# Five stages of a float32 decoder layer with other operand orders on TensorE

## The chip, the cores and the metric

The kernel runs on one core of one Trainium2 chip. A core has TensorE (PE, with its weight loads shown apart as PEld), VectorE (DVE), ScalarE (ACT), GpSimd (POOL) and SyncE (SP), which here issues the DMAs. The metric is device time in microseconds of one execution. The comparison that counts is the changed kernel against the kernel before, on the same chip.

## The reference

One layer of a hybrid decoder, float32, 256 tokens behind 16 learned meta tokens (272 columns in all), width 2048. What matters for this change is the chain of weight products:

```python
proj = xn @ w_in                      # q, k, v, gates of both branches
o_fox = forgetting_attention(...)     # 8 heads of 128
o_gla = gated_linear_attention(...)   # 4 heads, value width 512
y = sigmoid(gate_fox) * (o_fox @ w_o_fox) + sigmoid(gate_gla) * (o_gla @ w_o_gla)
h = h + y @ w_out
h = h + square(relu(xn2 @ w1)) @ w2   # w1: 2048 x 8192, w2: 8192 x 2048
out = rmsnorm(h)[16:]
```

All weights are used once, by 256 or 272 token columns, and come from HBM as float32.

## The kernel before

Everything is kept transposed: channels on the 128 partitions, tokens along the free dimension. A float32 value is split in two float32r parts, an upper part (hi) and the remainder (lo), and a product is hi·hi + hi·lo + lo·hi. The activations of a block of 128 channels lie as two runs in SBUF, hi tokens and lo tokens, with a gap that each operand sets for itself (AT_OG, AT_Y, AT_X2, AT_A); `x[k]` is a view of 128 x 2 x 256.

The weights come as blocks of 128 output channels by 2048 input channels (`stream()` lists them in order of use). `next_weights` loads one block in two halves of 8 input blocks: SP issues the DMA into `raw`, ScalarE casts it to `whi` (L120), VectorE subtracts to get `wlo` (L121). `raw`, `whi` and `wlo` have 5 buffers each, so up to two and a half blocks are prepared ahead of TensorE.

One output block of 128 channels is one `gemm2`: 16 input blocks, and for each one `mac2` (L135 to L137), which is two matmuls into one PSUM bank of 512 float32 columns. The first has `whi` as weights and streams both runs of the activations, 512 columns (hi·hi into columns 0 to 255, hi·lo into 256 to 511). The second has `wlo` as weights, streams the 256 hi columns and adds to columns 0 to 255. Each matmul has a weight load of its own. Here such two matmuls are called a pair. `total` or `add_residual` then adds the two halves of the bank with ScalarE and VectorE while TensorE is at the next block.

The stages that the change touches, in order of time:

- `gate()` is a `gemm2` over `xt` (the normalised input), with a sigmoid behind it. Four gates are made ahead, while the last steps of the attention heads (`later`, run by `issued()` after each product) are still open; the other 28 come in the loop over `j0`.
- In that loop each output block has one `gemm2` over `og` (the linear attention's output): 16 in all.
- The output projection: 16 `gemm2` over `y`.
- The MLP in four groups `g`: 16 `gemm2` over `x2` (first matrix; `relu2` squares the result and splits it into `a`), then 16 over `a` (second matrix). In group 3 the last NL = 4 output blocks of the second matrix are computed by code of their own, first all `wlo` products (L845), then the `whi` products for one half of the tokens after the other (L854: 2 x 128 columns).

The scheduler keeps each engine's instructions in the order of its own simulation of the program; the PE order is that of the code but for the `later` steps.

Of the kernel before, what the change touches and what calls it, by code (L numbers as in the profile page):

```python
# [16 lines left out]
P = 128  # L17
# [48 lines left out]
def trunk(ctx: ExitStack, tc: tile.TileContext, hT, w_small, w_all, consts, w_alpha2, out):  # L66
# [3 lines left out]
    def nm(s):  # L70
        serial[0] += 1
        return f"{s}_{serial[0]}"
# [35 lines left out]
    def weight_half(c, i, hi=None):  # L108
# [14 lines left out]
        return hi, lo, step  # L123

    def next_weights(keep_hi=None):
        c = chunk[0]
        chunk[0] += 1
        parts = []
        for i in range(2):
            hi, lo, step = weight_half(c, i, None if keep_hi is None else keep_hi[:, HK * i : HK * (i + 1), :])  # L130
            step(0, HK)
            parts.append((hi, lo))
        return lambda k: (parts[k // HK][0][:, k % HK, :], parts[k // HK][1][:, k % HK, :])
# [4 lines left out]

    def gemm2(w, x, k0=0, nk=KT):

        ps = bank(pg, "ps")
        for k in range(nk):
            hi, lo = w(k0 + k)
            mac2(ps, hi, lo, x[k], k == 0, k == nk - 1)
        issued()
        return ps
# [580 lines left out]

    def gate():
        t = total(gemm2(next_weights(), xt))
        nc.gpsimd.tensor_tensor(t, t, rbt, op=ALU.mult)  # L730
        s = late.tile([P, NT], F32, tag="gate", name=nm("gate"), bufs=6)
        nc.scalar.activation(s, t, AF.Sigmoid)
        return s

    ahead = [gate() for _ in range(4)]
    flush()
# [3 lines left out]
    for j0 in range(0, KT, 2):  # L740
# [5 lines left out]
        for j in range(2):  # L746
            t = total(gemm2(next_weights(), og))
            nc.vector.tensor_tensor(t, gates[2 * j + 1], t, op=ALU.mult)
            nc.vector.tensor_tensor(yf[:, j0 + j, :], gates[2 * j], t, op=ALU.add)
# [38 lines left out]
    for j in range(KT):  # L788
        add_residual(j, gemm2(next_weights(), y))
        nc.scalar.activation(x2[j][:, 0, :], ht[:, j, :], AF.Identity, scale=gain(1, j))  # L790
# [167 lines left out]
```

## Time and profile before

| what | value |
|---|---|
| median of the two runs shown | 1636.05 us (1634.11 to 1637.98) |
| span of the profiled execution | 1632.3 us, 3.75 us below that median |
| pairs in `mac2` | 3424 (1952 over x and x2, 960 over a, 256 over og, 256 over y, 128 of the attention's output), in a total of 9996 PE records |
| busy VectorE, ScalarE | 1033.6 us (63%), 788.5 us (48%) |
| HBM read | 289.19 MB, 178 GB/s over the span |

A row of the timeline gives start, length, engine, line, operation, output and inputs, their shapes, and how many instructions are merged. The length of a matmul in a row goes from its start to the modelled end, and matmuls overlap in the array; what one of them costs in a stream is the distance from its start to the start of the next. A row of the stages gives the length of the stage and each engine's busy time in it with the number of instructions. A row of the groups gives the total busy time, the mean in nanoseconds of one, and the idle time ahead of them with what ended it.

### The profile page before, as it was taken

What the parts mean: (1) busy time and instruction counts of PE and PEld (TensorE: products, weight loads), DVE (VectorE), ACT (ScalarE), POOL (GpSimd) and SP (SyncE); (2) the same over time, 40 slices, a digit from 0 to 9 for tenths busy, and PEclk for the clock granted to TensorE, in tenths of its full rate; (3) what the DMA queues carried; (4) which work ended last, traced back from release to release, by engine and by line L of the source; (5) the groups of instructions that cost most, each with busy time, mean ns of one, the idle gap of its engine ahead of it and who ended that gap; (6) DMA issues with size and microseconds to landing.
All of it is one profiled execution on the core that took longest, in us unless ns stands there. A gap on an engine that the chain in (4) does not pass through costs nothing.

```text
span 1632.3 us, 25617 instructions
## 1 busy us (share of the span) xinstructions
PE 1614.8 (99%) x9996; PEld 1448.8 (89%) x9996; DVE 1033.6 (63%) x1591; ACT 788.5 (48%) x1217; POOL 93.4 (6%) x146
## 2 busy tenths in 40 slices
PE   9999999999999999999999999999999999999997
PEld 7999999999998888888888888888888888888886
DVE  6767657476655555555677766566655776567655
ACT  6555444454445444444555444444444444444563
POOL 1000000010000000000011000000000000000022
PEclk9999999999999999999999999999999999999998
DMA  9444455455455565655555555655566656565662
GB/s 290 143 151 157 159 167 163 160 189 160 157 161 169 187 190 187 188 188 189 188 187 189 185 186 188 188 188 188 181 196 186 191 184 191 187 190 185 188 196 66
DMA packets 90266, 292.97 MB, mean 179 GB/s; under 512 B 9096, under 2 KB 21648, under 8 KB 89888
## 3 DMA queue, kind: packets, MB, share of 16 engines
q1 hardware_dynamic: 87552, 288.88, 55.8%
q8 instruction: 78, 1.28, 0.3%
q10 hardware_dynamic: 2416, 1.33, 0.3%
q0 software_dynamic: 176, 1.12, 0.2%
q14 instruction: 44, 0.36, 0.1%
HBM read 289.19 MB, written 2.11 MB: 178 GB/s over the span
## 4 chain that ended last, share of the span: by engine, by line
PE 97%; DVE 1%; DMA 1%; ACT 0%; issue 0%; SPq 0%; DVEq 0%; ACTq 0%
PE ps L136 50%; PE ps L137 26%; PE psa L155 5%; PE psa L154 5%; PE psa L153 5%; PE ps L854 1%; PE ps L339 1%; DMA h<-hT_dram 1%; PE pa L501 1%; PE ps L845 0%; PE ps L346 0%; PE po L565 0%; DMA raw<-w_all_dram 0%; PE pz L399 0%; PE po L566 0%; PE pq L663 0%
## 5 line engine op out<-in xcount | busy, mean ns | idle before, releaser
L121 DVE TENSOR_TENSOR wlo<-raw,whi 128x1024 fp32r<-128x1024 f32 x522 | 639.9, 1226 | 502.9 <-ACT whi L120 501.3
L120 ACT CAST whi<-raw 128x1024 fp32r<-128x1024 f32 x522 | 547.6, 1049 | 750.9 <-PE ps L136 507.0
L136 PE MATMUL ps<-x,whi 128*128 128x512 f32 x1952 | 688.2, 396 | 0.0
L137 PE MATMUL ps<-x,wlo 128*128 128x256 f32 x1952 | 549.5, 282 | 0.0
L136 PEld LDWEIGHTS ps<-x,whi 128*128 128x128 f32 x1952 | 367.0, 188 | 84.1
L137 PEld LDWEIGHTS ps<-x,wlo 128*128 128x128 f32 x1952 | 368.8, 189 | 0.0
L136 PE MATMUL ps<-a,whi 128*128 128x512 f32 x960 | 336.3, 395 | 0.0
L137 PE MATMUL ps<-a,wlo 128*128 128x256 f32 x960 | 268.5, 280 | 0.0
L136 PEld LDWEIGHTS ps<-a,whi 128*128 128x128 f32 x960 | 180.0, 188 | 42.2
L153 PE MATMUL psa<-x,whi 128*128 128x272 f32 x640 | 187.1, 292 | 2.1 <-DVE ri L196 2.1
L154 PE MATMUL psa<-x,wlo 128*128 128x272 f32 x640 | 184.9, 289 | 0.0
L155 PE MATMUL psa<-x,whi 128*128 128x272 f32 x640 | 184.8, 289 | 0.0
L137 PEld LDWEIGHTS ps<-a,wlo 128*128 128x128 f32 x960 | 181.2, 189 | 0.4
L153 PEld LDWEIGHTS psa<-x,whi 128*128 128x128 f32 x640 | 120.4, 188 | 2.8 <-issue 2.1
L154 PEld LDWEIGHTS psa<-x,wlo 128*128 128x128 f32 x640 | 120.5, 188 | 0.2
L155 PEld LDWEIGHTS psa<-x,whi 128*128 128x128 f32 x640 | 120.6, 188 | 0.1
L136 PE MATMUL ps<-og,whi 128*128 128x512 f32 x256 | 90.3, 395 | 0.0
L136 PE MATMUL ps<-y,whi 128*128 128x512 f32 x256 | 89.8, 395 | 0.0
L766 POOL TENSOR_TENSOR acc<-acc,hsq 128x256 f32<-128x256 f32 x26 | 29.5, 1134 | 775.6 <-ACT hsq L765 775.6
L137 PE MATMUL ps<-og,wlo 128*128 128x256 f32 x256 | 71.8, 281 | 0.0
L137 PE MATMUL ps<-y,wlo 128*128 128x256 f32 x256 | 71.7, 281 | 0.0
L165 DVE TENSOR_TENSOR evt<-ps,evb 128x256 f32<-128x256 f32 x158 | 66.1, 418 | 0.0
(262 smaller groups left out, 1387.0 us busy)
## 6 DMA issues: line engine op xcount, KB each, us to landing
raw<-w_all_dram SPq DMA_DIRECT2D x537, 512.0 KB, 4.3
raw<-w_all_dram SPq DMA_DIRECT2D x7, 384.0 KB, 6.3
h<-hT_dram SPq DMA_DIRECT2D x1, 1100.0 KB, 10.0
negc<-fdram POOLq DMA_DIRECT2D x1, 1088.0 KB, 6.0
out_dram<-h SPq DMA_DIRECT2D x3, 256.0 KB, 2.6
out_dram<-h ACTq DMA_DIRECT2D x3, 256.0 KB, 3.1
h<-hT_dram SPq DMA_DIRECT2D x1, 550.0 KB, 7.3
raw<-w_all_dram SPq DMA_DIRECT2D x2, 256.0 KB, 4.4
```

What stands on the lines that cost most here:

```text
L120: nc.scalar.copy(hi[:, k, :], r)
L121: nc.vector.tensor_tensor(lo[:, k, :], r, hi[:, k, :].bitcast(F32), op=ALU.subtract)
L136: nc.tensor.matmul(ps, hi, x, start=first, stop=False)
L137: nc.tensor.matmul(ps[:, 0:NT], lo, x[:, 0, :], start=False, stop=last)
L153: nc.tensor.matmul(ps[:, 0:n], hi, x[:, k, 0, :], start=(k == 0), stop=False)
L154: nc.tensor.matmul(ps[:, 0:n], lo, x[:, k, 0, :], start=False, stop=False)
L155: nc.tensor.matmul(ps[:, 0:n], hi, x[:, k, 1, :], start=False, stop=(k == KT - 1))
L165: nc.vector.tensor_tensor(t, ps[:, 0:NT], b, op=ALU.add)
L339: nc.tensor.matmul(ps, hi, x[:, k, :, NM:NA], start=st, stop=False)
L501: nc.tensor.matmul(dst, k[:, a, :], q[:, a, :], start=(a == 0), stop=(a == 1))
L766: nc.gpsimd.tensor_tensor(acc, acc, sq, op=ALU.add)
L854: nc.tensor.matmul(ps[:, NT:], w(k)[0], a[k][:, :, tok], start=(k == 0), stop=(k == KT - 1))
```

## The change

Products, inputs and outputs stay the same; each of five stages forms them in another order.

- The four gates made ahead use `mac2_halves`: per input block four matmuls, for each half of the tokens one of 2 x 128 columns with `whi` and one of 128 columns with `wlo`. The weights are loaded in the order hi, lo, hi, lo.
- The products over `og` use `gemm2_runs`: for each half of the weights, first the eight matmuls of 512 columns with `whi`, then the eight of 256 with `wlo`.
- The output projection uses `mac2_thirds`: three matmuls of 256 columns (hi·hi, hi·lo, lo·hi), with `whi` loaded twice.
- MLP group 1 uses `mac2_back`: both matmuls stream their columns from the last to the first, and write the PSUM columns from the last to the first.
- MLP group 2 uses `mac2_lo_back`: only the `wlo` matmul goes backwards.
- MLP group 3 (but for the last four output blocks) uses `paired_weights`: the hi and lo weights of an input block lie in one tile, alternating element by element, so that ScalarE and VectorE write, and the weight loads read, every second element. The tiles are cut so that each of the two tags holds four input blocks with both parts, and a half is made by two casts and two subtractions of 512 elements in place of one each of 1024. The DMAs are the same.

```diff
+    def paired_weights():
+        c = chunk[0]
+        chunk[0] += 1
+        parts = []
+        for i in range(2):
+            raw = wp.tile([P, HK * P], F32, tag="raw", name=nm("raw"), bufs=RAW)
+            nc.sync.dma_start(raw, w_all[c][:, i * HK * P : (i + 1) * HK * P])
+            r = raw.rearrange("p (q k m) -> p q k m", q=2, m=P)
+            for q, tag in enumerate(("whi", "wlo")):
+                t = wp.tile([P, HK // 2, P, 2], F32R, tag=tag, name=nm(tag))
+                nc.scalar.copy(t[:, :, :, 0], r[:, q])
+                nc.vector.tensor_tensor(t[:, :, :, 1], r[:, q], t[:, :, :, 0].bitcast(F32), op=ALU.subtract)
+                parts.append(t)
+        return lambda k: tuple(parts[k // 4][:, k % 4, :, o] for o in range(2))
...
+    def mac2_back(ps, hi, lo, x, first, last):
+        nc.tensor.matmul(ps[:, ::-1], hi, x[:, ::-1, ::-1], start=first, stop=False)
+        nc.tensor.matmul(ps[:, NT - 1 :: -1], lo, x[:, 0, ::-1], start=False, stop=last)
+
+    def mac2_lo_back(ps, hi, lo, x, first, last):
+        nc.tensor.matmul(ps, hi, x, start=first, stop=False)
+        nc.tensor.matmul(ps[:, NT - 1 :: -1], lo, x[:, 0, ::-1], start=False, stop=last)
+
+    def mac2_halves(ps, hi, lo, x, first, last):
+        both = ps.rearrange("p (o t) -> p o t", t=NT)
+        for i in range(2):
+            t = slice(P * i, P * (i + 1))
+            nc.tensor.matmul(both[:, :, t], hi, x[:, :, t], start=first and i == 0, stop=False)
+            nc.tensor.matmul(ps[:, t], lo, x[:, 0, t], start=False, stop=last and i == 1)
+
+    def mac2_thirds(ps, hi, lo, x, first, last):
+        nc.tensor.matmul(ps[:, 0:NT], hi, x[:, 0, :], start=first, stop=False)
+        nc.tensor.matmul(ps[:, NT:], hi, x[:, 1, :], start=False, stop=False)
+        nc.tensor.matmul(ps[:, 0:NT], lo, x[:, 0, :], start=False, stop=last)
+
+    def gemm2_runs(w, x):
+        ps = bank(pg, "ps")
+        for k0 in range(0, KT, HK):
+            for k in range(k0, k0 + HK):
+                nc.tensor.matmul(ps, w(k)[0], x[k], start=(k == 0), stop=False)
+            for k in range(k0, k0 + HK):
+                nc.tensor.matmul(ps[:, 0:NT], w(k)[1], x[k][:, 0, :], start=False, stop=(k == KT - 1))
+        issued()
+        return ps
...
-    ahead = [gate() for _ in range(4)]
+    ahead = [gate(mac2_halves) for _ in range(4)]
...
-            t = total(gemm2(next_weights(), og))
+            t = total(gemm2_runs(next_weights(), og))
...
-        add_residual(j, gemm2(next_weights(), y))
+        add_residual(j, gemm2(next_weights(), y, mac=mac2_thirds))
...
+        weights, mac = ((next_weights, mac2), (next_weights, mac2_back), (next_weights, mac2_lo_back), (paired_weights, mac2))[g]
...
-            ps = gemm2(next_weights(), x2)
+            ps = gemm2(weights(), x2, mac=mac)
...
-            add_residual(j, gemm2(next_weights(), a))
+            add_residual(j, gemm2(weights(), a, mac=mac))
```

`gemm2` and `gate` take the form as an argument (`mac`).

Two places show it in the engines' programs. The first is on PE, where the last attention head ends (`pof` is its output, `pq` the scores of the next) and the first gate made ahead begins (`ps`). Before:

```order
L184 MATMUL pof_5514<-pah_5424,val_5365 128x256
L714 MATMUL pof_5514<-pT_5295,vb_5294 128x144
L715 MATMUL pof_5514<-pc_3631,vc_3627 128x16
L663 MATMUL pq_5522<-fk_5297,fq_5298 128x144
L136 MATMUL ps_5551<-x,whi_5540 128x512
L137 MATMUL ps_5551<-x,wlo_5541 128x256
```

And in the changed kernel:

```order
L229 MATMUL pof_5514<-pah_5424,val_5365 128x256
L759 MATMUL pof_5514<-pT_5295,vb_5294 128x144
L760 MATMUL pof_5514<-pc_3631,vc_3627 128x16
L708 MATMUL pq_5522<-fk_5297,fq_5298 128x144
L166 MATMUL ps_5551<-x,whi_5540 128x2x128
L167 MATMUL ps_5551<-x,wlo_5541 128x128
```

What surrounds the gate stays where it was; the pair has become smaller matmuls, which appear twice per input block.

The second place is on ScalarE, where the weights of MLP group 3 begin to be prepared, still during the second matrix of group 2 (`evb` is the copy in `add_residual`). Before:

```order
L770 COPY evb_14227<-ps_14194 128x256
L120 CAST whi_14336<-raw_14335 128x1024
L120 CAST whi_14380<-raw_14379 128x1024
L770 COPY evb_14276<-ps_14243 128x256
L120 CAST whi_14386<-raw_14385 128x1024
L120 CAST whi_14434<-raw_14433 128x1024
```

And in the changed kernel:

```order
L120 CAST whi_14720<-raw_14719 128x1024
L135 CAST whi_14765<-raw_14763 128x512
L815 COPY evb_14660<-ps_14627 128x256
L135 CAST wlo_14768<-raw_14763 128x512
L135 CAST whi_14773<-raw_14771 128x512
L135 CAST wlo_14776<-raw_14771 128x512
```

One cast per half has become two of half the length, the second into a buffer of the tag `wlo`; the copies out of PSUM keep their places among the halves.

More of the change, by code (lines that the diff above doesn't have):

```diff
@@ L137, in mac2, with gemm2 @@
         nc.tensor.matmul(ps[:, 0:NT], lo, x[:, 0, :], start=False, stop=last)
-    def gemm2(w, x, k0=0, nk=KT):
+    def mac2_back(ps, hi, lo, x, first, last):
[23 more added lines that the diff above has]
+        return ps
+    def gemm2(w, x, k0=0, nk=KT, mac=mac2):
         ps = bank(pg, "ps")
@@ L143, in gemm2 @@
             hi, lo = w(k0 + k)
-            mac2(ps, hi, lo, x[k], k == 0, k == nk - 1)
+            mac(ps, hi, lo, x[k], k == 0, k == nk - 1)
         issued()
@@ L725, in trunk, with gate @@
         fox_head(hd)
-    def gate():
-        t = total(gemm2(next_weights(), xt))
+    def gate(mac=mac2):
+        t = total(gemm2(next_weights(), xt, mac=mac))
         nc.gpsimd.tensor_tensor(t, t, rbt, op=ALU.mult)
```

## The prediction

> **What bounds the kernel now.** I read the page first: engine shares, slices, and the chain that ended last.
>
> ```profile
> span 1632.3 us, 25617 instructions
> ...
> PE 1614.8 (99%) x9996; PEld 1448.8 (89%) x9996; DVE 1033.6 (63%) x1591; ACT 788.5 (48%) x1217; POOL 93.4 (6%) x146
> ...
> PEclk9999999999999999999999999999999999999998
> ...
> PE 97%; DVE 1%; DMA 1%; ACT 0%; issue 0%; SPq 0%; DVEq 0%; ACTq 0%
> ```
>
> TensorE is the chain. Its busy share alone would not say so, because matmul ends are modelled; the chain does, with 97% of the span, and the granted clock gives no slack to win back. Then the table of waits, for the two engines that prepare the weights:
>
> ```profile
> ACT whi L120 <- PE ps L136: 507.0, 340, 3.9
> DVE wlo L121 <- ACT whi L120: 501.3, 470, 3.7
> ```
>
> ScalarE waits 507 us in total for TensorE to hand back a weight buffer, and VectorE 501 us for ScalarE. The suppliers are ahead of the consumer, so the change is priced by what it does to the pace of matmuls. The stages that it touches, by the table of busy times by stretch (a gate loop, the products over og, the projection, MLP groups 1 and 2, and the two matrices of group 3):
>
> ```profile
> 573.52:595.92 22.40, 22.40 (x130) 19.64 (x129) 11.99 (x14) 10.42 (x15) 2.21 (x3) 1.00 0.58 187
> 562.27:573.52 11.25, 11.25 (x67) 9.82 (x65) 7.27 (x10) 4.74 (x6) 0.00 (x0) 1.00 0.55 187
> 808.68:898.47 89.79, 89.79 (x515) 78.60 (x514) 64.53 (x82) 49.31 (x80) 13.48 (x14) 1.00 0.59 187
> 1078.92:1258.53 179.61, 179.61 (x1027) 156.84 (x1026) 114.90 (x160) 80.65 (x112) 0.00 (x0) 1.00 0.60 188
> 1258.53:1438.13 179.60, 179.60 (x1026) 156.84 (x1025) 114.91 (x160) 80.66 (x112) 0.00 (x0) 1.00 0.60 188
> 1438.13:1528.02 89.89, 89.89 (x514) 78.50 (x513) 62.82 (x94) 42.47 (x63) 0.00 (x0) 1.00 0.60 187
> 1528.02:1595.31 67.29, 67.29 (x386) 58.77 (x385) 39.20 (x50) 42.31 (x64) 13.44 (x10) 1.00 0.60 189
> ```
>
> PE is busy in every microsecond of them (first two columns equal). Divided by their pairs: 22.40/64 = 0.350 us for the gates, 11.25/32 = 0.352 for og, 89.79/256 = 0.351 for the projection, 179.61/512 = 0.351 in groups 1 and 2, 89.89/256 and 67.29/192 = 0.351 in group 3. Inside a pair, by the timeline of PE (start, length, line, operation):
>
> ```profile
> 1099.96 0.39 PE L136 MATMUL ps<-x,whi 128*128 128x512 f32 x1
> 1100.19 0.28 PE L137 MATMUL ps<-x,wlo 128*128 128x256 f32 x1
> 1100.31 0.39 PE L136 MATMUL ps<-x,whi 128*128 128x512 f32 x1
> ```
>
> From start to start the 512 columns take 0.23 and the 256 columns 0.12 us: time follows the columns, about 0.457 ns each.
>
> Three rows price the smaller matmuls: the end of the kernel, which has long series of 256 columns (L845 one run with wlo, L854 two runs of 128 with whi), and the attention heads, which have the smallest shapes.
>
> ```profile
> 1595.31 5.86 PE L845 MATMUL ps<-a,wlo 128*128 128x256 f32 x48
> 1601.01 1.80 PE L854 MATMUL ps<-a,whi_last 128*128 128x256 f32 x14
> ...
> 1604.78 8.46 PE L854 MATMUL ps<-a,whi_last 128*128 128x256 f32 x70
> 1613.08 0.28 PE L872 MATMUL pn<-ones,acc 128*128 128x1 f32 x2
> ```
>
> 48 in 5.70 us are 0.1188 each, 70 in 8.30 us are 0.1186 each, every one with a weight load of its own.
>
> ```profile
> 365.55 0.27 PE L701 MATMUL pt<-cons,pr 128*128 128x128 f32 x1
> ...
> 365.99 0.27 PE L705 MATMUL pu<-cons,pr 128*16 128x128 f32 x1
> ...
> 372.25 0.27 PE L183 MATMUL pof<-pal,vah 128*128 128x256 f32 x1
> 372.36 0.28 PE L184 MATMUL pof<-pah,val 128*128 128x256 f32 x1
> 372.48 0.41 PE L714 MATMUL pof<-pT,vb 128*128 128x144 f32 x2
> 372.73 0.29 PE L715 MATMUL pof<-pc,vc 128*128 128x16 f32 x2
> ...
> 372.61 0.31 PEld L715 LDWEIGHTS pof<-pc,vc 128*128 128x128 f32 x2
> 372.84 0.30 PEld L663 LDWEIGHTS pq<-fk,fq 128*128 128x128 f32 x2
> ```
>
> Four transposes of 128 columns take 0.44, 0.11 each. A plain float32 product of 144 columns takes 0.25 (two records). Two weight loads of 128 columns take 0.23, although the products beside them have only 16 columns: a weight load cannot be paced faster than about 0.115, and a lo matmul of 0.119 hides the next one with almost nothing to spare.
>
> **The change, part by part.**
>
> *Gates.* 64 pairs of 0.350 become 64 times two hi matmuls of 2 x 128 columns at 0.1186 (the L854 row is this very shape on the reading side) and two lo matmuls of 128 columns. For the latter no row has float32r. Lower end: half of a 256-column one, 0.059, if the weight loads were free; 2 x (0.1186 + 0.059) = 0.355, +0.3 us in all. Upper end: the plain float32 pace, 0.25/144 x 128 = 0.222; 2 x 0.3406 = 0.681, +21.2 us. I take 0.11, the transposes, nearest in columns and near the pace of the weight loads that here come one per matmul: 2 x 0.2286 = 0.457, +0.107 x 64 = +6.8 us. It lies on the path, since nothing on PE waits in this stage; the `later` steps of the last head only get more time.
>
> *Runs.* The same 256 + 256 matmuls. In a run of eight lo matmuls each weight load must hide under one of 256 columns instead of 512; the L845 row is such a run, at 0.1188 against 0.12 in the pair. Price 0, between -0.5 and +0.5 us (0.002 x 256). If the cover failed and a load of 0.115 lay bare once per lo matmul, it would be +29 us, which that row excludes. The wlo half is asked for later and the whi half handed back earlier, both on the safe side.
>
> *Thirds.* 256 pairs of 0.3507 become three matmuls of 0.1188: 0.3564, +0.0057 x 256 = +1.4 us, between 0 (time by columns alone) and +1.6 (0.119 each). The additional weight loads hide as in the L845 row.
>
> *Backwards.* 512 pairs wholly, 512 in the lo matmul only; no instruction more. No row has a descending operand, so the bounds are rows of pace: above, the 128-column transposes, 0.11/128 = 0.859 ns per column; below, the 0.11 us in which L183 streams 256, 0.43 ns. With 0.859 group 1 pays (768 x 0.859 ns - 0.351) x 512 = +158 us and group 2 (0.220 - 0.118) x 512 = +52 us; with 0.43 they gain 0.021 x 512 = 10.7 and 0.008 x 512 = 4.1 us. I take 0: the columns, lines and banks touched are the same ones, only in descending order, and the nearest row is the same pair ascending.
>
> *Interleaved weights.* 448 pairs; more instructions for ScalarE and VectorE, by the groups:
>
> ```profile
> L120 ACT CAST whi<-raw 128x1024 fp32r<-128x1024 f32 x522 | 547.6, 1049 | 750.9 <-PE ps L136 507.0 <-issue 148.3 <-PE psa L155 84.3
> L287 ACT CAST whi<-raw 128x768 fp32r<-128x768 f32 x7 | 5.8, 832 | 3.9 <-PE ps L339 3.0 <-DMA raw<-w_all_dram 0.9
> ...
> L121 DVE TENSOR_TENSOR wlo<-raw,whi 128x1024 fp32r<-128x1024 f32 x522 | 639.9, 1226 | 502.9 <-ACT whi L120 501.3 <-issue 0.4
> L288 DVE TENSOR_TENSOR wlo<-raw,whi 128x768 fp32r<-128x768 f32 x7 | 6.7, 956 | 3.5 <-PE ps L346 3.0 <-ACT whi L287 0.6
> ```
>
> Going on from 1024 and 768 to 512 elements gives 0.615 for a cast and 0.686 for a subtraction: per block 4 x 0.615 = 2.46 us on ScalarE (2.10 before) and 4 x 0.686 = 2.74 on VectorE (2.45). In the first matrix of group 3 VectorE goes from 62.82 to 67.5 us of 89.89, ScalarE from 42.47 to 48.2: still hidden behind PE. Should VectorE handle every second element at half its pace, a subtraction costs 1.226, the stage needs 62.82 + 16 x 2.45 = 102 us of VectorE, and the cover is gone: +12 us there and +1.3 in the second matrix. The weight load now reads every second element. If its pace stays 0.115, nothing; if it doubles to 0.23, the lo matmul no longer covers the next load and each pair grows by 0.23 - 0.12 = 0.11, +49 us. I take 0, since the nearest row, the same load of as many columns, is below the matmul it hides under. The page "SBUF — State Buffer" of the Trainium skill (Specifications) says that a 16-byte line needs at least two accesses for full bandwidth; steps of two float32 just meet that, so by the page the sum would be the same 0. No trace here shows it.
>
> Sum: 6.8 + 0 + 1.4 + 0 + 0 = +8.2 us on a span of 1632.3, so 1640.5; with the 3.75 us between the span and the median of the runs shown, 1644.3. Its own range, with the gates' ends and the bounds of thirds and runs, is 1636 to 1659.
>
> **The rivals.**
>
> *Descending columns cost time (slower).* Place: every matmul of group 1, and the lo one in group 2. Price: up to +158 and +52 us, 1644 + 210 = 1854. It decides from about 0.504 ns per descending column on (0.457 now): 0.047 ns x (768 + 256) x 512 = 24.6 us, which with the 8.2 is 2%. For it speaks that PE has nothing to hide it behind; against it, that the matmul of two runs (L854) pays nothing for its jump, so the order of addresses is not all that sets the pace. The page "PSUM — Partial Sum Buffer" of the Trainium skill (Specifications) says that lines there have 8 bytes and any non-contiguous pattern slows matmuls significantly; if a descending run counts as such, this rival is what it gives. No run so far has such an output.
>
> *Interleaving costs time.* Through VectorE +13.5 us, 1658; through the weight loads +49 us, 1693. For it: loads of 0.115 have only about 4 ns of cover under the lo matmul. Against: the suppliers' large waits, and that the load's pace goes by columns.
>
> *The orders do nothing at all,* the gates included: the 128-column lo matmuls cost half of the 256. Then about 1636. Against it stand the two weight loads in 0.23.
>
> *Faster.* If a changed order let all 2048 pairs stream at 0.43 ns, it would be 2048 x 0.021 = 43 us less, 1644 - 43 = 1601. Only one row has that pace.
>
> **How the numbers follow.** Forecast 0.58, 1644; descending columns at the full price 0.18, 1854; interleaving, or a small part of the descending price, 0.18, from 1658 to 1693, of which 0.12 beyond 2%; nothing at all 0.04, 1636; faster 0.02, 1601. The range 1632 to 1700 takes in the first, third and fourth case, 0.80, its upper end the third case with some of the gates' upper end. By a bound of 2% (33 us, about what a measurement of this kernel can tell from no change): faster 0.02, same 0.58 + 0.06 + 0.04 = 0.68, slower 0.18 + 0.12 = 0.30.
>
> **What would show it.** In the changed trace: the gates' four matmuls in 0.457 us per input block; og and the projection within 2% of 0.351; groups 1 and 2 179.6 us each; group 3 without waits of PE for VectorE, and its pairs at 0.351. A gate step near 0.68 would put the 128-column float32r matmul at the plain float32 pace; a group 1 far above 180 us while group 2 grows by a third as much would be the descending rival; a lo matmul of 0.23 in group 3 alone the weight-load one. The forecast is wrong if any of the three large stages changes its pace by more than a few per cent.

## The result, and the profile after

| what | before | after |
|---|---|---|
| median of the runs shown | 1636.05 us (1634.11 to 1637.98) | 1644.68 us (1643.66 to 1645.69) |
| ratio, with its 95% interval | | 1.0054 (1.0036 to 1.0071) |
| span of the profiled execution | 1632.3 us | 1644.0 us |

The change makes the kernel slower by about half a per cent: 0.0054 x 1636 = 8.8 us, with 5.9 to 11.6 as the interval. The page of the changed kernel (busy time of the engines, chain that ended last) looks as before:

```profile
PE 1625.1 (99%) x10380; PEld 1475.8 (90%) x10380; DVE 1038.1 (63%) x1647; ACT 804.1 (49%) x1273; POOL 90.8 (6%) x146
...
PE 98%; DVE 1%; DMA 1%; ACT 0%; issue 0%; SPq 0%; DVEq 0%; ACTq 0%
```

TensorE is still the chain, now with 384 matmuls more (256 in the projection, 128 in the gates). So the time is found by cutting TensorE's timeline at the first matmul of each stage. The busy times by stretch, for the stages in the order of the prediction (gates, one stretch of products over `og`, projection, MLP groups 1 and 2, the two matrices of group 3). Columns: stretch, length, busy time and instructions of PE, PEld, DVE, ACT and POOL, granted clock, DMA share, GB/s:

```profile
495.37:526.98 31.61, 31.61 (x277) 31.55 (x276) 13.65 (x24) 13.47 (x26) 2.19 (x3) 1.00 0.41 134
571.89:583.11 11.22, 11.22 (x67) 9.79 (x66) 7.21 (x10) 5.49 (x7) 0.00 (x0) 1.00 0.57 193
818.11:908.87 90.76, 90.76 (x770) 90.76 (x769) 64.49 (x82) 48.44 (x80) 13.81 (x14) 1.00 0.58 188
1089.36:1270.27 180.91, 180.91 (x1026) 157.34 (x1025) 114.86 (x160) 80.58 (x112) 0.00 (x0) 1.00 0.57 186
1270.27:1449.49 179.22, 179.22 (x1027) 156.70 (x1025) 114.95 (x164) 81.44 (x116) 0.00 (x0) 1.00 0.58 188
1449.49:1539.55 90.06, 90.06 (x515) 80.67 (x513) 65.41 (x127) 53.50 (x96) 0.00 (x0) 1.00 0.56 188
1539.55:1607.10 67.55, 67.55 (x386) 60.50 (x385) 41.67 (x70) 45.80 (x82) 9.13 (x10) 1.00 0.58 187
```

And of the kernel before, the stretch of the four gates made ahead (with the few steps of the last head that stand among them) and 8 us in the front part, long before any changed instruction:

```profile
52.00:56.00 4.00, 2.98 (x23) 3.02 (x24) 3.78 (x18) 1.49 (x4) 0.00 (x0) 1.00 0.80 258
56.00:60.00 4.00, 4.00 (x34) 4.00 (x33) 2.01 (x5) 1.71 (x2) 0.00 (x0) 1.00 0.06 14
492.94:517.53 24.59, 24.59 (x148) 21.76 (x148) 13.57 (x24) 13.16 (x26) 2.22 (x3) 1.00 0.54 170
```

No stage has a wait of PE (its first two columns stay equal), so each difference is one of pace. The gates grow by 31.61 - 24.59 = 7.02 us, and their PEld column goes from 21.76 of 24.59 to 31.55 of 31.61: weight loads now fill the whole stretch. A full column alone prices nothing, since the projection's is full too (90.76 of 90.76) and the projection grows by 0.97 only; experiments 3 and 4 price it. Group 1 grows by 1.30, group 3 by 0.17 and 0.26; group 2 loses 0.38; a stretch of `og` loses 0.03. Together that is +9.3 us with the gates and the projection, inside the measured interval.

The spans differ by 11.7, and the remaining 2.4 us stand ahead of the first changed instruction: the gates begin at 495.37 where they began at 492.94, with the same program up to there. The same 8 us of the changed kernel's front part:

```profile
52.00:56.00 4.00, 2.06 (x9) 2.09 (x10) 3.96 (x15) 1.82 (x6) 0.00 (x0) 0.75 0.52 157
56.00:60.00 4.00, 4.00 (x29) 4.00 (x28) 1.69 (x11) 1.05 (x1) 0.00 (x0) 0.83 0.29 105
```

In both executions PE had just waited 2.08 us for VectorE; behind that wait the granted clock was 0.75 and 0.83 in this one and 1.00 in the other. That makes 1.5 of the 2.4 us. The other 0.9 came before, behind a wait for ScalarE at 22.4 us (2.99 us long here, 1.28 in the kernel before): from 22.4 to 50 us the granted clock was 0.94 here and 1.00 there. Kernels of the experiments that have the front part and the gates of before show both (from 52 to 56 us 0.63 in experiment 6 and 1.00 in experiment 5), so it belongs to the execution and not to the change. This is why the difference is taken stage by stage here.

### The profile page after: what moved, and what is told of

It reads as the page before. It is cut to its first block, busy times and chain, and to the rows that moved or that the text cites. A ratio compares the mean times of both kernels' runs of the same rounds, so it can differ in the third digit from the quotient of the medians.

```text
span 1644.0 us, 26514 instructions
## 1 busy us (share of the span) xinstructions
PE 1625.1 (99%) x10380; PEld 1475.8 (90%) x10380; DVE 1038.1 (63%) x1647; ACT 804.1 (49%) x1273; POOL 90.8 (6%) x146
## 4 chain that ended last, share of the span: by engine, by line
PE 98%; DMA 1%; DVE 1%; ACT 0%; issue 0%; SPq 0%; DVEq 0%; ACTq 0%
PE ps L151 28%; PE ps L152 14%; PE ps L155 7%; PE ps L159 7%; PE psa L200 5%; PE psa L199 5%; PE psa L198 5%; PE ps L156 4%; PE ps L160 4%; PE ps L178 4%; PE ps L171 2%; PE ps L180 2%; PE ps L172 2%; PE ps L170 2%; PE ps L166 1%; PE ps L384 1%
## 5 line engine op out<-in xcount | busy, mean ns | idle before, releaser
L121 DVE TENSOR_TENSOR wlo<-raw,whi 128x1024 fp32r<-128x1024 f32 x466 | 571.0, 1225 | 458.5 <-ACT whi L120 456.5
L120 ACT CAST whi<-raw 128x1024 fp32r<-128x1024 f32 x466 | 488.8, 1049 | 681.5 <-PE ps L151 233.2
L151 PE MATMUL ps<-x,whi 128*128 128x512 f32 x1248 | 441.9, 396 | 0.0
L152 PE MATMUL ps<-x,wlo 128*128 128x256 f32 x1248 | 351.6, 282 | 0.0
L151 PEld LDWEIGHTS ps<-x,whi 128*128 128x128 f32 x1248 | 235.4, 189 | 51.9
L152 PEld LDWEIGHTS ps<-x,wlo 128*128 128x128 f32 x1248 | 236.6, 190 | 0.0
L151 PE MATMUL ps<-a,whi 128*128 128x512 f32 x352 | 124.5, 395 | 0.0
L152 PE MATMUL ps<-a,wlo 128*128 128x256 f32 x352 | 98.4, 280 | 0.0
L155 PE MATMUL ps<-a,whi 128*128 128x512 f32 x256 | 90.5, 397 | 0.0
L155 PE MATMUL ps<-x,whi 128*128 128x512 f32 x256 | 90.4, 398 | 0.0
L159 PE MATMUL ps<-a,whi 128*128 128x512 f32 x256 | 89.8, 395 | 0.0
L159 PE MATMUL ps<-x,whi 128*128 128x512 f32 x256 | 89.4, 394 | 0.0
L151 PEld LDWEIGHTS ps<-a,whi 128*128 128x128 f32 x352 | 66.7, 190 | 14.8
L156 PE MATMUL ps<-x,wlo 128*128 128x256 f32 x256 | 72.2, 282 | 0.0
L156 PE MATMUL ps<-a,wlo 128*128 128x256 f32 x256 | 72.0, 282 | 0.0
L171 PE MATMUL ps<-y,whi 128*128 128x256 f32 x256 | 71.9, 281 | 0.0
```

Of the source, the lines that this page charges most:

```text
L120: nc.scalar.copy(hi[:, k, :], r)
L121: nc.vector.tensor_tensor(lo[:, k, :], r, hi[:, k, :].bitcast(F32), op=ALU.subtract)
L151: nc.tensor.matmul(ps, hi, x, start=first, stop=False)
L152: nc.tensor.matmul(ps[:, 0:NT], lo, x[:, 0, :], start=False, stop=last)
L155: nc.tensor.matmul(ps[:, ::-1], hi, x[:, ::-1, ::-1], start=first, stop=False)
L156: nc.tensor.matmul(ps[:, NT - 1 :: -1], lo, x[:, 0, ::-1], start=False, stop=last)
```

## The experiments

What was to be told apart: for the gates, whether the pace of the weight loads or the gap in the PSUM write costs; for the descending stages, why group 1 lost and group 2 gained; and for the orders that cost nothing, how far one can go before they do.

**1 and 2. The gates alone.** In the changed kernel the gates made ahead become pairs again; in the kernel before they alone become halves.

```diff
-    ahead = [gate(mac2_halves) for _ in range(4)]
+    ahead = [gate() for _ in range(4)]
```

> The changed kernel with the four gates made ahead as pairs again; the other four stages stay changed. Theory (the gates' half-token products are nearly all of the difference): the trace gave the gate stage 7.0 us, so 1644.7 - 7.0 = 1637.7, 1.001 of the kernel before, and the gate stage back at 24.6 us. Rival (the other four stages, or the first 490 us, carry several microseconds too): 1640 or more, 1.0025 and up.

> The kernel before with only the four gates made ahead by half tokens. Theory: 1636.05 + 7.0 = 1643, 1.0043 of the kernel before. Rival (the other stages carry half of it): about 1640, 1.0025.

Measured: 1636.84 us without the gates' halves, ratio to the kernel before 1.0011 (1.0002 to 1.0020); 1644.57 with them alone, 1.0046 (1.0033 to 1.0059). The gates hold most of the result, and the other four stages together about 0.1%. In experiment 1 the first and second matrix of group 1 took 90.33 and 90.58, of group 2 89.39 and 89.82; in the changed kernel's trace 90.34 and 90.57, 89.39 and 89.83. Differences of some tenths of a microsecond in a stage repeat from execution to execution, so they may be read.

**3 and 4. What in the gates costs.** All 32 gates of the kernel before are changed: in one kernel only the `whi` matmul is cut in two of 2 x 128 columns, in the other only the `wlo` matmul in two of 128.

```diff
+    def mac2_hi_split(ps, hi, lo, x, first, last):
+        both = ps.rearrange("p (o t) -> p o t", t=NT)
+        for i in range(2):
+            t = slice(P * i, P * (i + 1))
+            nc.tensor.matmul(both[:, :, t], hi, x[:, :, t], start=first and i == 0, stop=False)
+        nc.tensor.matmul(ps[:, 0:NT], lo, x[:, 0, :], start=False, stop=last)
...
+    def mac2_lo_split(ps, hi, lo, x, first, last):
+        nc.tensor.matmul(ps, hi, x, start=first, stop=False)
+        for i in range(2):
+            t = slice(P * i, P * (i + 1))
+            nc.tensor.matmul(ps[:, t], lo, x[:, 0, t], start=False, stop=last and i == 1)
```

> The kernel before, all 32 gates (512 pairs) with the hi product in two of 2 x 128 columns, each written to PSUM as two runs with a gap, and the lo product whole; three weight loads. Theory W (a product costs its columns at 0.457 ns or one weight load of 0.116 us, whichever is longer): 3 x 0.1188 = 0.356 per pair, +0.006 x 512 = +3 us. Rival G (the write in two runs is what costs, 0.17 us per product as the slots of the changed kernel read, and 128 lo columns cost 0.06): 2 x 0.1725 + 0.118 = 0.463, +0.113 x 512 = +58 us.

> The kernel before, all 32 gates (512 pairs) with the hi product whole and the lo product in two of 128 columns, each with its weight load; no gap in any output. Theory W: 0.234 + 2 x 0.116 = 0.466 per pair, +0.116 x 512 = +59 us. Rival G: 0.234 + 2 x 0.06 = 0.354, +2 us.

Measured: 1638.84 and 1690.94 us beside 1636.16 for the kernel before, +2.7 and +54.8, one execution each; by the lengths of its eight gate stretches the first is +4.8 (7 x 0.61 and 0.48). The stretch of four gates in the loop, first with `whi` cut, then with `wlo` cut (22.40 before):

```profile
534.88:557.89 23.01, 23.01 (x195) 23.01 (x193) 12.00 (x14) 10.43 (x15) 2.21 (x3) 1.00 0.52 184
```

```profile
542.79:571.95 29.16, 29.16 (x194) 26.27 (x193) 11.99 (x14) 10.43 (x15) 2.19 (x3) 1.00 0.43 146
```

Both have 192 matmuls and as many loads. With three of 256 columns a block takes 23.01/64 = 0.360 us, hardly more than the pair's 0.350, though the `whi` products write two runs with a gap, so the gap costs next to nothing. With 512, 128 and 128 it takes 0.456; with 0.234 for the 512 columns, (0.456 - 0.234)/2 = 0.111 is left for each product of 128, nearly the 0.118 of one of 256. Single starts don't show this (in the changed kernel's gates the next start follows a product of 2 x 128 after 0.17 us and one of 128 after 0.06), so a price is read over a whole block, or off the loads. In experiment 4 the loads (start, length, line):

```profile
549.98 0.19 PEld L140 LDWEIGHTS ps<-x,whi 128*128 128x128 f32 x1
550.09 0.42 PEld L143 LDWEIGHTS ps<-x,wlo 128*128 128x128 f32 x2
550.43 0.19 PEld L140 LDWEIGHTS ps<-x,whi 128*128 128x128 f32 x1
```

The first `wlo` load comes 0.11 behind the `whi` load; the two `wlo` loads take 0.34, which is the 0.234 of the 512 columns and 0.11 again. The changed kernel's own gates:

```profile
505.96 0.19 PEld L166 LDWEIGHTS ps<-x,whi 128*128 128x128 f32 x1
506.06 0.19 PEld L167 LDWEIGHTS ps<-x,wlo 128*128 128x128 f32 x1
506.19 0.19 PEld L166 LDWEIGHTS ps<-x,whi 128*128 128x128 f32 x1
506.30 0.19 PEld L167 LDWEIGHTS ps<-x,wlo 128*128 128x128 f32 x1
506.42 0.19 PEld L166 LDWEIGHTS ps<-x,whi 128*128 128x128 f32 x1
```

Four loads in 0.46 us, 0.115 each, one behind the other. By its columns alone such a block would take 768 x 0.457 ns = 0.351. Theory W holds in both runs and rival G falls.

These two runs leave one rival, because each of their matmuls brings a load of 128 columns: that a matmul costs at least 0.111 whatever its load. The linear attention's scores in the kernel before (L501, plain float32) have products of 64 columns behind loads of 80 and of 64 columns (128*80 and 128*64 in the rows):

```profile
90.67 0.45 PE L501 MATMUL pa<-qd,ke 128*80 128x64 f32 x4
90.95 0.62 PE L501 MATMUL pa<-r,ke 128*80 128x128 f32 x4
...
91.78 0.40 PE L501 MATMUL pa<-qd,ke 128*64 128x64 f32 x4
92.01 0.22 PE L501 MATMUL pa<-r,ke 128*64 128x64 f32 x1
```

Four take 0.28 us with the loads of 80 and 0.23 with the loads of 64, so 0.070 and 0.058 each. Therefore 0.111 is no floor of a matmul, and the same product is slower behind the longer load. 0.070 behind 80 columns is 0.875 ns per column of the load, which for 128 gives 0.112.

**5. Descending, in parts.** In the kernel before, group 0 reads its columns descending and writes ascending, group 1 reads ascending and writes descending, group 2 does both (the sums of the first two groups thus stand mirrored in tokens).

```diff
+    def mac2_read_back(ps, hi, lo, x, first, last):
+        nc.tensor.matmul(ps, hi, x[:, ::-1, ::-1], start=first, stop=False)
+        nc.tensor.matmul(ps[:, 0:NT], lo, x[:, 0, ::-1], start=False, stop=last)
+
+    def mac2_write_back(ps, hi, lo, x, first, last):
+        nc.tensor.matmul(ps[:, ::-1], hi, x, start=first, stop=False)
+        nc.tensor.matmul(ps[:, NT - 1 :: -1], lo, x[:, 0, :], start=False, stop=last)
...
-            ps = gemm2(next_weights(), x2)
+            ps = gemm2(next_weights(), x2, mac=(mac2_read_back, mac2_write_back, mac2_back, mac2)[g])
```

> The kernel before, with the MLP's groups 0, 1 and 2 partly backwards: group 0 reads its activations from last to first and writes upwards, group 1 reads upwards and writes PSUM from last to first, group 2 does both as group 1 of the changed kernel; group 3 as before. In groups 0 and 1 the tokens of each product come out mirrored, so the numbers are not the reference's. Stages before: 180.45, 179.61 and 179.60 us. Theory (descending costs nothing by itself; the +1.3 us of the changed kernel's group 1 comes with the particular operand positions of reading): group 1 within 0.3 of 179.6, groups 0 and 2 each 1 to 1.5 above. Rival (writing backwards costs it): groups 1 and 2 each 1 to 1.5 above, group 0 unchanged. Second rival (chance of one execution): all three within 0.3.

Measured: 1636.5 us beside 1637.4, one execution each. A second matrix of the kernel before, and the stretches of this one: second matrix of group 0 (read descending), both matrices of group 1 (written descending), first matrix of group 2 (both):

```profile
989.20:1078.92 89.72, 89.72 (x515) 78.37 (x513) 52.08 (x66) 38.18 (x49) 0.00 (x0) 1.00 0.59 187
```

```profile
989.57:1080.14 90.57, 90.57 (x514) 78.82 (x513) 52.07 (x66) 38.22 (x49) 0.00 (x0) 1.00 0.55 186
1080.14:1259.75 179.61, 179.61 (x1026) 156.71 (x1025) 114.91 (x160) 80.75 (x112) 0.00 (x0) 1.00 0.55 188
1259.75:1350.09 90.34, 90.34 (x514) 78.50 (x513) 62.81 (x94) 42.47 (x63) 0.00 (x0) 1.00 0.55 187
```

Writing descending takes 179.61, exactly what group 1 took before. Reading descending takes 90.57 over `a` where 89.72 stood, and both together take in group 2 what reading alone does (90.34 and 90.57). The small loss is all on the reading side, as the theory said. Why it is 0.5% over `x2` and 0.95% over `a` this run doesn't say. Nor does it say why group 2 of the changed kernel, with the `wlo` matmul alone descending, gained: 0.50 over `x2` (89.39 after 89.89), with a loss of 0.10 over `a`. No run varied that.

**6 and 9. How far apart columns may lie.** The operand `a` of the second matrices is laid out anew, with the products unchanged. In experiment 6 its columns lie 2, 4 and 8 elements apart in groups 0, 1 and 2 (hi and lo of one or more blocks interleaved element by element):

```diff
+    def alternating(step):
+        t = keep.tile([P, S1], F32R, tag="s1", name=nm("a"))
+        r = t[:, 0 : KT * 2 * NT].rearrange("p (b t s) -> p b s t", s=step, t=NT)
+        n = step // 2
+        return [r[:, k // n, 2 * (k % n) : 2 * (k % n) + 2, :] for k in range(KT)]
...
-        a = operand(keep, "a", S1, AT_A, "s1")
+        a = alternating(2 << g) if g < 3 else operand(keep, "a", S1, AT_A, "s1")
```

> The kernel before, with the activations a of the MLP's second matrix laid out alternating: the streamed columns lie 2, 4 and 8 float32 apart in groups 0, 1 and 2 (before: 1). Same arithmetic. Second-matrix stages before: 89.7 us each. Theory L (lines of 16 bytes, two columns per line suffice): 89.7 at step 2, then up to twice that at steps 4 and 8, where every column is a line of its own: about 180 us each. Rival N (time follows the number of columns, wherever they lie): 89.7 in all three. Rival M (any step above 1 halves the pace): 180 in all three.

Measured: 1885.39 us beside 1637.4. The second matrices of groups 0, 1 and 2 (89.7 each before):

```profile
991.03:1165.13 174.10, 174.10 (x514) 106.65 (x513) 52.15 (x66) 38.15 (x50) 0.00 (x0) 1.00 0.29 100
1255.05:1433.18 178.13, 178.13 (x515) 107.19 (x513) 52.48 (x67) 38.40 (x49) 0.00 (x0) 1.00 0.29 98
1523.11:1689.49 166.38, 166.38 (x515) 105.22 (x514) 52.59 (x67) 38.39 (x50) 0.00 (x0) 1.00 0.31 104
```

Steps of two already halve the pace, and larger ones cost about the same, as rival M said. Experiment 9 lays hi and lo in alternating runs: of two columns in group 0, of two columns but one element later in group 1, of four in group 2.

```diff
+    def in_runs(how):
+        u, off = how
+        t = keep.tile([P, S1], F32R, tag="s1", name=nm("a"))
+        r = t[:, off : off + KT * 2 * NT].rearrange("p (b t s u) -> p b s t u", s=2, t=NT // u, u=u)
+        return [r[:, k] for k in range(KT)]
...
+        a = in_runs(((2, 0), (2, 1), (4, 0))[g]) if g < 3 else operand(keep, "a", S1, AT_A, "s1")
```

> The kernel before, with the activations a of the MLP's second matrix in short runs, hi and lo alternating: runs of 2 columns (8 bytes) starting at a multiple of 8 bytes in group 0, the same runs starting 4 bytes later in group 1, runs of 4 columns in group 2. Same arithmetic. Second-matrix stages before: 89.7 us; with columns 2 apart (e6) 174. Theory P (TensorE fetches the streamed operand by two neighbouring float32 at a time, whatever follows): 89.7 in groups 0 and 2; in group 1 also 89.7 if the two need only be neighbours, about 174 if they must share an aligned 8 bytes. Rival (any interruption of an unbroken run halves the pace): 174 in groups 0 and 1, between in group 2.

Measured: 1804.36 us beside 1634.49. The same three stretches:

```profile
989.18:1163.28 174.10, 174.10 (x514) 106.64 (x513) 52.14 (x66) 38.16 (x50) 0.00 (x0) 1.00 0.30 100
1253.19:1429.82 176.63, 176.63 (x515) 106.35 (x513) 52.13 (x66) 38.20 (x50) 0.00 (x0) 1.00 0.29 99
1519.73:1608.49 88.76, 88.76 (x514) 77.76 (x513) 52.05 (x66) 38.14 (x49) 0.00 (x0) 1.00 0.56 190
```

Two neighbours are no better than none: 174.10 both times, so theory P falls. Four (16 bytes of float32) keep the pace, and even gain 1% on the layout of before, one run of hi and one of lo; so the rival, which let any interruption cost, holds for runs of two alone. For this operand the reading of 16 bytes with two elements used, which the page "SBUF — State Buffer" of the Trainium skill (Specifications) calls enough for full bandwidth, is half the pace; the measurement decides.

**7. How far apart weights may lie.** Weights 2 elements apart in group 1 (as in group 3 of the changed kernel) and 4 apart in group 2, with plain pairs.

```diff
-            ps = gemm2(next_weights(), x2)
+            ps = gemm2((apart_weights(1 << g) if g in (1, 2) else next_weights()), x2, mac=mac2)
...
-            add_residual(j, gemm2(next_weights(), a))
+            add_residual(j, gemm2((apart_weights(1 << g) if g in (1, 2) else next_weights()), a, mac=mac2))
```

> The kernel before, with the weights of MLP group 1 lying 2 elements apart as in group 3 of the changed kernel, and those of group 2 lying 4 apart (two input blocks with both parts per tile). Same arithmetic; ScalarE and VectorE write with the same steps, in 128 x 256 pieces in group 2. Stages before: 179.6 us each. Theory L (a weight load slows where each 16-byte line holds one element): group 1 180.5, group 2 with loads of 0.23 us, 0.234 + 0.23 = 0.464 per pair, 238 us. Rival N (a load takes the same for any step): 180.5 and 181. If PE is seen waiting for VectorE or ScalarE in group 2, the stage says nothing on the loads.

Measured: 1697.99 us. Group 1 took 180.1, group 2 240.5. The first matrix of group 2, and the loads in it (the names of the two weight tiles no longer tell hi from lo: each tile holds both):

```profile
1261.63:1381.85 120.22, 120.22 (x515) 120.22 (x513) 95.99 (x192) 80.95 (x159) 0.00 (x0) 1.00 0.42 142
```

```profile
1300.03 0.31 PEld L154 LDWEIGHTS ps<-x,whi 128*128 128x128 f32 x1
1300.24 0.33 PEld L155 LDWEIGHTS ps<-x,whi 128*128 128x128 f32 x1
1300.50 0.31 PEld L154 LDWEIGHTS ps<-x,whi 128*128 128x128 f32 x1
```

Two loads now take 0.47 us, 0.235 each, twice the 0.115; VectorE and ScalarE are busy 96 and 81 of 120 us and PE doesn't wait for them. So a load reads every second element at full pace and every fourth at half. Theory L holds (0.470 per pair where 0.464 was expected). Full pace means here that the load stays under the 0.118 of the 256 columns that cover it. For weights the sentence of the page "SBUF — State Buffer" of the Trainium skill (Specifications) holds, where it fails for the other operand.

**8. Gaps in the output.** Three products of 256 columns, written to PSUM in runs of two columns (group 1) and of eight (group 2) with gaps of the same length.

```diff
+    def apart_view(ps, n):
+        return ps.rearrange("p (t o u) -> p o t u" if n else "p (o t u) -> p o t u", o=2, u=n or 2)
+
+    def runs(v, n):
+        return v.rearrange("p (t u) -> p t u", u=n or 2)
+
+    def mac2_apart2(ps, hi, lo, x, first, last, n=2):
+        two = apart_view(ps, n)
+        for o in range(2):
+            nc.tensor.matmul(two[:, o], hi, runs(x[:, o, :], n), start=first and o == 0, stop=False)
+        nc.tensor.matmul(two[:, 0], lo, runs(x[:, 0, :], n), start=False, stop=last)
```

> The kernel before, with three products of 256 columns per input block in MLP groups 1 and 2, each written to PSUM in runs of 2 columns (group 1) or 8 columns (group 2) with gaps as long between them. Same arithmetic. Stages before 179.6; three products of 0.1188 per pair are 182.5. Theory N (time follows the columns, the gaps in the output cost nothing): 182 to 184 in both. Rival (a non-contiguous output slows a matmul significantly, as the Trainium skill's page PSUM — Partial Sum Buffer says): group 1 at least a third longer, 240 us or more, group 2 between.

Measured: 1639.02 us beside 1637.4, one execution each. The two groups:

```profile
1081.51:1262.23 180.72, 180.72 (x1538) 180.72 (x1537) 114.78 (x160) 80.70 (x112) 0.00 (x0) 1.00 0.56 187
1262.23:1442.96 180.73, 180.73 (x1538) 180.73 (x1537) 114.79 (x160) 80.68 (x112) 0.00 (x0) 1.00 0.55 186
```

180.7 with either gap, 0.118 per matmul: three products in place of two cost 1.1 us per group of 512 pairs, no more than in the projection (0.97 for 256 pairs, without gaps), so the gaps cost nothing. Theory N holds; single columns with gaps were not tried. The rule of the page "PSUM — Partial Sum Buffer" of the Trainium skill (Specifications), that any non-contiguous pattern slows matmuls significantly, isn't borne out by runs of two columns or more, nor by descending ones (experiment 5).

**10. Quarters.** The four gates made ahead in quarters of the tokens: 2 x 64 columns with `whi`, 64 with `wlo`.

```diff
+    def mac2_quarters(ps, hi, lo, x, first, last):
+        both = ps.rearrange("p (o t) -> p o t", t=NT)
+        for i in range(4):
+            t = slice(C * i, C * (i + 1))
+            nc.tensor.matmul(both[:, :, t], hi, x[:, :, t], start=first and i == 0, stop=False)
+            nc.tensor.matmul(ps[:, t], lo, x[:, 0, t], start=False, stop=last and i == 3)
```

> The kernel before, with the four gates made ahead by quarters of the tokens: per input block four hi products of 2 x 64 columns and four lo products of 64, eight weight loads. Theory W (one weight load of about 0.114 us sets the pace of every product shorter than 250 columns): 8 x 0.114 = 0.91 per pair, +0.56 x 64 = +36 us against before. Rival (a product has a fixed cost of its own and then its columns; from the halves, 0.465 per pair over four products, (0.465 - 0.351)/2 = 0.057 for each of the two added): 0.351 + 6 x 0.057 = 0.69, +22 us.

Measured: 1715.67 us in one execution, +81: neither theory. Two stretches from the gates on, with PE busy throughout and PEld for all but 0.6 us, and the granted clock third from the end:

```profile
498.00:500.00 2.00, 2.00 (x20) 2.00 (x20) 0.04 (x1) 0.00 (x0) 0.00 (x0) 1.00 0.03 10
504.00:600.00 96.00, 96.00 (x448) 95.38 (x449) 10.92 (x16) 12.32 (x21) 2.18 (x3) 0.50 0.11 38
```

And loads of that kernel at the full and at the halved clock:

```profile
497.84 0.19 PEld L143 LDWEIGHTS ps<-x,whi 128*128 128x128 f32 x1
497.95 0.19 PEld L144 LDWEIGHTS ps<-x,wlo 128*128 128x128 f32 x1
...
529.83 0.33 PEld L143 LDWEIGHTS ps<-x,whi 128*128 128x128 f32 x1
530.05 0.33 PEld L144 LDWEIGHTS ps<-x,wlo 128*128 128x128 f32 x1
530.26 0.33 PEld L143 LDWEIGHTS ps<-x,whi 128*128 128x128 f32 x1
```

In the first 9 us (from 492.8 on) a load takes 0.11, as the load's pace demands; from 502.2 on the clock is at 0.50 and a load takes 0.213. It stays so to the end of the gates at 597.3 and for 3.6 us of ordinary pairs; then the loads are back at their old distances. The theory of the load's pace priced its own part rightly and missed the clock, which cost the larger part.

**11. Runs everywhere.** The one order that seemed to gain (8 matmuls with `whi`, then 8 with `wlo`) for every pair of the kernel before.

```diff
-        for k in range(nk):
-            hi, lo = w(k0 + k)
-            mac2(ps, hi, lo, x[k], k == 0, k == nk - 1)
+        for at in range(0, nk, HK):
+            for k in range(at, at + HK):
+                nc.tensor.matmul(ps, w(k0 + k)[0], x[k], start=(k == 0), stop=False)
+            for k in range(at, at + HK):
+                nc.tensor.matmul(ps[:, 0:NT], w(k0 + k)[1], x[k][:, 0, :], start=False, stop=(k == nk - 1))
```

> The kernel before, with every product that is made by pairs formed as the changed kernel forms those over og: eight hi products, then eight lo products. Theory (the run saves about 1 ns per pair, from 11.25 to 11.22 us per 32 pairs in the og stage): -1 ns x 3424 = -3.4 us, 0.998 of the kernel before. Rival (the og stage's difference is chance): within 0.5 us, 1.000.

Measured: 1635.47 beside 1634.49 us, ratio 1.0002 (0.9993 to 1.0011): no gain. The projection took 89.46 (-0.33), first matrices 90.08 (+0.19), second ones 89.59 (-0.13), and the stretch of `og` itself 11.26 where it was 11.25 before and 11.22 in the changed kernel. So the saving of 0.03 doesn't go with this order alone. (The pairs are 3552, not 3424, with the 128 of the attention's output; at 1 ns each that is -3.6 us in place of -3.4.)

**12. Runs of four columns everywhere.** The layout that gained 1% in experiment 9, for `og`, `y`, `x2` and `a`.

```diff
+    U = 4
...
+        r = t[:, 0 : KT * 2 * NT].rearrange("p (b t o u) -> p b o t u", o=2, t=NT // U, u=U)
+        return [r[:, k] for k in range(KT)]
```

> The kernel before, with its moving operands og, y, x2 and a laid out in runs of four columns of the upper parts and four of the lower parts in turn, where they were halves of a buffer or alternating columns; products, weights and gates are those of before. Theory R (a moving operand read in runs of four columns goes at a slightly better pace whatever operand it is): in the runs with columns in runs, group 2's second matrix took 88.76 us where it took 89.71, 0.95 us or 1.06% less. og, y and the eight MLP stages together are about 900 us of TensorE time, so some 9.5 us less: ratio 0.994, and each second matrix at 88.8. Rival S (the gain belongs to where that one buffer lay in that group, or to a alone): 1 to 4 us less, ratio 0.9975 to 0.9995, and the stages of og, y and x2 as before (og 11.25 per 32 pairs, y 89.8, first matrices 89.9). A third outcome, that writing the runs costs the casts more than is covered, would show as PE waiting for DVE or ACT at the starts of groups.

Measured: 1634.0 beside 1634.72 us, ratio 0.9991 (0.9982 to 1.0000), within the range that the rival gave and far from 0.994. The span of its profiled execution is 1630.2, 2.1 below that of the kernel before. The stretches of `og`, `y`, a second and a first matrix:

```profile
562.41:573.70 11.29, 11.29 (x66) 9.86 (x65) 7.27 (x10) 4.74 (x6) 0.00 (x0) 1.00 0.53 183
809.14:897.90 88.76, 88.76 (x515) 77.80 (x513) 64.43 (x82) 49.33 (x80) 13.37 (x14) 1.00 0.57 192
989.20:1077.96 88.76, 88.76 (x515) 77.77 (x513) 52.07 (x66) 38.15 (x49) 0.00 (x0) 1.00 0.57 190
1077.96:1168.41 90.45, 90.45 (x515) 78.98 (x513) 62.82 (x94) 42.47 (x63) 0.00 (x0) 1.00 0.55 186
```

`y` and `a` gain 1.03 and 0.96 us, `x2` loses 0.56, `og` loses 0.04 per stretch of 32 pairs. With one and the same layout a pair takes 88.76/256 = 0.3467 us over `y` and `a`, and 90.45/256 = 0.3533 over `x2` and 11.29/32 = 0.3528 over `og`. `y` and `a` share one buffer (tag s1), `og` and `x2` another (s2). The work beside it doesn't part them: VectorE and ScalarE are busy for 64.4 and 49.3 us over `y`, and for 62.8 and 42.5 over `x2`. So the theory that the gain goes with the layout whatever the operand falls, and its rival is right in size and in that the gain belongs to one buffer, but not in that the other stays as it was. The two prices nearly cancel. Runs of four in the first buffer alone would by these stretches be worth 1.03 + 3 x 0.96 + 0.72 = 4.6 us (0.72 from the last second matrix, 66.57 after 67.29); that wasn't tried.

## Why the prediction came out, point by point

| step of the prediction | said | measured in the stages |
|---|---|---|
| gates, 128-column product at 0.11 | +6.8 | +7.02 |
| runs over `og` | 0 | -0.03 per stretch; the loop with all of it 291.15, then 291.13 |
| thirds in the projection | +1.4 | +0.97 |
| backwards, groups 1 and 2 | 0 | +1.30 and -0.38 |
| interleaved weights, group 3 | 0 | +0.43 |
| sum | +8.2 | +9.3 |
| time | 1644.3 | 1644.68 |

*The gates* were the term that mattered, and the value chosen between +0.3 and +21.2 was the right one. The prediction took 0.11 from the transposes, "near the pace of the weight loads that here come one per matmul". The second half of this is the reason: experiments 3 and 4 show that it is the loads, 0.111 per product of 128 columns. The transposes agree by luck: two of them (L704, L705) load 16 columns and not 128, and take 0.11 all the same, so their pace is not their loads'. And of the two loads in 0.23 the first (0.12) had the product of 144 columns ahead of it to wait for (L714, 0.12 too); only the second (0.11) went at the load's own pace. Both ends were wrong in a telling way: the columns alone (0.059) would need loads that are free, and the plain float32 pace doesn't apply to float32r.

*Runs:* price 0, within its bounds of 0.5 us. Experiment 11 shows that the order gains nothing over all pairs.

*Thirds:* a size slightly off. 90.76/768 = 0.1182 per matmul where 0.1188 was taken from the L845 row; 0.0006 x 768 is the difference of 0.4.

*Backwards:* the price 0 was off by 1.30 and -0.38 us, 0.92 together, and the rival of descending columns falls. It needed 0.047 ns more per column to reach 2%; reading `a` descending costs 0.85 us over 256 x 768 columns, 0.004 ns. The prediction's reason, that "the columns, lines and banks touched are the same ones", holds for writing to the last digit (179.61), and for reading to 1%. That group 1's loss and group 2's gain partly cancel is luck. What the remaining half to one per cent is stays open; experiment 12 shows differences of that size (0.347 against 0.353 us per pair) between two buffers with one layout, so it may be the place that is read and not the order as such. That was not isolated.

*Interleaved weights:* the price 0 was within 0.5 us, and the cover was named rightly: no wait of PE for VectorE or ScalarE in group 3. The suppliers' own prices were a little low, and with them the load on ScalarE: 53.50 us in the first matrix where 48.2 was said (VectorE: 65.41, where 67.5 was said). The groups of the changed kernel (line, engine, operation, output and input, shapes, count | busy, mean ns | idle before, and what ended it):

```profile
L136 DVE TENSOR_TENSOR wlo<-raw,wlo 128x512 fp32r<-128x512 f32 x56 | 39.0, 696 | 14.7 <-ACT wlo L135 14.6
L136 DVE TENSOR_TENSOR whi<-raw,whi 128x512 fp32r<-128x512 f32 x56 | 38.7, 691 | 24.8 <-ACT whi L135 24.8
L135 ACT CAST whi<-raw 128x512 fp32r<-128x512 f32 x56 | 37.3, 665 | 35.2 <-PE ps L152 27.6 <-PE ps L159 7.6
```

A subtraction of 512 took 0.691 to 0.696 (0.686 was said), a cast 0.665 (0.615 was said), and VectorE did not halve its pace, which was the prediction's first worry. Its second, a weight load that doubles, is real but two elements further on: every fourth element, not every second (experiment 7), and then costs what the prediction had worked out (0.11 per pair; here 0.470 - 0.351 = 0.12).

*The time:* the medians differ by 8.6 us and the stages by 9.3 where 8.2 was forecast. That the forecast of the time itself is nearer still (1644.3 and 1644.68) has some luck in it: the stages are 1.1 us above the forecast, and the front part, which the prediction has as unchanged, lost 2.4 us to a lower clock in the profiled execution; its span stands only 0.7 us below the median, where 3.75 was taken.

## What to carry to other kernels

Price a matmul as the longer of its own columns and the next weight load, and read the price over a whole block: here a product of 128 columns cost no less than 0.111 us, so a product may be cut only down to the length that covers a load (256 columns: 0.118 beside 0.111 to 0.115). The order in which columns are written is free here, descending and with gaps between runs of two or more, while the moving operand kept its pace in runs of four float32 (16 bytes) and lost half of it in runs of two, and a weight load kept its pace two float32 apart and took twice as long four apart. Where an engine shows as busy throughout, cut its timeline at the stages and compare their lengths: they repeat to some hundredths of a microsecond and show effects that the whole time hides.

## What the runs showed of the hardware that was not expected

- The granted clock halved with PE never waiting, in the one execution of experiment 10: 0.50 for some 98 us while loads stood back to back and the array streamed for little of the time (experiment 10: 768 x 0.457 ns = 0.35 us of columns in a block of 0.89 us at full clock, 39%). In the halves it is 0.351 of 0.46, 76%, and the clock stayed at 1.00. That the share decides is a guess. In experiment 6 the same columns filled 0.351 of 0.680 us (174.10/256), 52%, for 174 us at a clock of 1.00; if the share decides, its limit lies lower. The page "TensorE: Matmul & The Clock Gate" of the Trainium skill (Part 1) puts the half rate down to idle windows of about 3.4 us; no wait of that length is in these rows, unless a mostly unfed array counts as idle.
- A float32r moving operand with steps of two, or runs of two, goes at half the pace (174.1 against 89.7 us), with runs of four at full pace (88.8); a weight load of every second element at full pace, of every fourth at half (0.235 against 0.115 us).
- One layout has two paces in two buffers: 0.3467 and 0.3533 us per pair. What in their place does it stays open.
